# A decoder block in fp32: the FFN's result is transposed from its SBUF tiles, and operands of the last stage are asked for earlier

## The chip, the cores and the metric

The kernel runs on one core of a Trainium2 chip. The metric is the device time of one execution in microseconds; the median of several timed runs counts. Times inside an execution come from one profiled run and are counted from the start of its span.

## The reference

One layer of a hybrid decoder, sequence length 2048, width 1024, FFN width 2816, one batch, all fp32. The change lies behind the mixing part, in the last five lines.

```python
u = rmsnorm(h, attn_pre_norm)
... # gated linear recurrence and stick-breaking attention
h = h + rmsnorm(mix, attn_post_norm)
u = rmsnorm(h, ffn_pre_norm)
gate, up = split(u @ w_gate_up, [D_FF])
y = (silu(gate) * up) @ w_down
h = h + rmsnorm(y, ffn_post_norm)                 # called h2 below
out = h + (p @ ple_proj) * sigmoid(h @ ple_gate)  # called PLE below
```

## The kernel before

Every fp32 product is made of three matmuls of split operands: each operand `raw` is cast on ScalarE to a high part (`wh`, `uh`) and a low part `raw - high` is made on VectorE or GpSimd (`wl`, `ul`); `mm3` (lines 223 to 225) multiplies high by high, high by low, low by high. Tokens stand in four groups of 512 (0 to 3), a group in four token tiles of 128. The FFN and PLE matrix products work on a pair of groups at a time, with a scheme of seven block products in place of eight (`CHAIN`, in the order 1, 2, 6, 3, 7, 5, 4), so every operand exists as seven sums or differences of blocks.

`Drive` runs six stages one after the other: gate/up for groups 0 and 1 (stage 0), down (1), gate/up for groups 2 and 3 (2), down (3), PLE for groups 0 and 1 (4, the first PLE stage or first half) and PLE for groups 2 and 3 (5, the second half). A down stage has 77 steps of 12 matmuls, a gate/up stage 77 of 24, a PLE stage 36 of 12: seven products of four steps, then eight steps (`run_p`) that multiply `pt` by `ple_proj`. Before a step's matmuls, `Drive` has already issued the loads and casts (`prepare`) of steps 3 to 5 ahead. A hook `at(stage, step, f)` issues `f` right behind the matmuls of that step.

The order on TensorE is that of the code, word for word. On the other engines a scheduler fixes it when the program is built; at run time each engine takes its instructions in that order, so one that waits holds all behind it. Every DMA is issued by SyncE (SP in the rows). All loads of the last five stages go into one ring of ten buffers of 256 KB (`wr`, `load`, line 764).

Around the change:
- In a down stage, product 5 completes the result of the even group (0, 2) at step 65, product 4 that of the odd one (1, 3) at step 76. `ready[g][i]` holds the two halves of token tile `i`, SBUF tiles named `c` or `cu`.
- `post_y(g, i)` (line 1040) makes h2 of one token tile in place: sum of squares on ScalarE, 1/rms on GpSimd, scale by `gy` (a broadcast load of `ffn_post_norm`) on VectorE (line 1046), addition of the residual `hr` on GpSimd (line 789 by `add`), write to `h2_s` (line 1049; the rows print it `h_s`). It is hooked at stage 1 from step 67, stage 2 from step 0, stage 3 from step 67 and stage 4 from step 0.
- `turn` (line 696) loads rows of `h2_s` again (line 703, four blocks of 256 columns), transposes 128x128 blocks on TensorE (line 715), four to a PSUM bank `hg`, copies the bank on ScalarE (line 719) and writes 512 tokens of one feature block to `h2t_s` (line 722). Groups 0 and 1 are turned in stage 2, group 2 at stage 4 from step 2, group 3 from step 11.
- `s_part` (line 874) reads `h2t_s` and makes the operands of the second PLE half: part 0 those of products 1, 2 and 6, part 1 the other four. It is hooked at stage 4, steps 21, 23, 25, 27 (part 0) and 28 to 31 (part 1).
- `prepare_p` loads `ple_proj` and `pt`, and its casts need buffers `w` (eight in all) that the products before them still use.

Of the kernel before, what the change touches and what calls it, by code (L numbers as in the profile page):

```python
# [15 lines left out]
P = 128  # L16
T = 2048
D = 1024
ND = D // P
GT = 512  # L20
NG = T // GT
TT = GT // P
# [66 lines left out]
def hybrid_block(  # L89
# [6 lines left out]
    nc = tc.nc  # L96
    ctx.enter_context(tc.manual_schedule(engines={mybir.EngineType.PE}))
    x, p, out = x[0], p[0, 0], out[0]
# [6 lines left out]
    def scratch(name, shape):  # L105
        return [dram.tile(list(shape), F32, tag=f"{name}{g}", name=f"{name}{g}") for g in range(NG)]
# [9 lines left out]
    h2_s = scratch("h2_s", (GT, D))  # L116
    un_s = scratch("un_s", (GT, D))
    u_s = scratch("u_s", (ND, P, GT))
    h2t_s = scratch("h2t_s", (ND, P, GT))
# [9 lines left out]
    def ctile(name, shape, dt=F32, pool=const):  # L129
        return pool.tile(list(shape), dt, tag=name, name=name)  # L130

    ident = ctile("ident", (P, P))
# [40 lines left out]
    def bank(tag):  # L173
        return ps.tile([P, 512], F32, tag=tag, name=tag, bufs=BANKS[tag])
# [97 lines left out]
    def row_rstd(halves):  # L272
        ss = const.tile([P, 2], F32, tag="ss", name="ss", bufs=8)
        for j, y in enumerate(halves):
            nc.scalar.activation(junk, y, AF.Square, accum_out=ss[:, j:j + 1])
        r = const.tile([P, 1], F32, tag="ssum", name="ssum", bufs=8)
        nc.gpsimd.tensor_tensor(r, ss[:, 0:1], ss[:, 1:2], op=ALU.add)
        return rstd_of(const, r, D)
# [417 lines left out]
    def turn(src, dst, gain, tag, new_in, new_out):  # L696

        def get(q):
            ts = []
            for i in range(2):  # L700
                r = new_in().rearrange("p (t d) -> p t d", t=2)
                rows = src[2 * i * P:2 * (i + 1) * P, q * 256:(q + 1) * 256]
                nc.sync.dma_start(r, rows.rearrange("(t p) d -> p t d", p=P))
                ts += [r[:, 0, :], r[:, 1, :]]
            return ts

        nxt = get(0)
        yield
        for q in range(4):
            ts = nxt  # L710
            nxt = get(q + 1) if q < 3 else None
            for c in range(2):
                b = bank(tag)
                for t in range(TT):
                    nc.tensor.transpose(b[:, t * P:(t + 1) * P], ts[t][:, c * P:(c + 1) * P], ident)
                e = new_out()
                k = 2 * q + c
                if gain is None:
                    nc.scalar.copy(e, b)
                else:  # L720
                    nc.scalar.activation(e, b, AF.Copy, scale=gain[:, k:k + 1])
                nc.sync.dma_start(dst[k], e)
                yield
# [36 lines left out]
    def slot(tag, side, name, dt=F32):  # L760
        side = side if big[side] is not None else 0
        return big[side].tile([P, GT], dt, tag=f"{tag}{side}", name=name, bufs=SLOTS[tag.rstrip("hl")][side])

    def load(src, shape=None):
        r = slot("wr", 0, "wr")
        nc.sync.dma_start(r if shape is None else shape(r), src)
        return r

    def acc(name="acc"):
        turns["acc"] += 1  # L770
        return slot("acc", 0 if turns["acc"] % 3 == 0 else 1, name)

    def pair_of(src, kind, prod, lo_engine):
        if kind == "u":
            side = 0 if prod in (1, 2, 6) else 1
        else:
            turns["w"] += 1
            side = turns["w"] % 2
        hi = slot(kind + "h", side, kind + "h", F32R)
        lo = slot(kind + "l", side, kind + "l", F32R)  # L780
        nc.scalar.copy(hi, src)  # L781
        lo_engine.tensor_tensor(lo, src, hi.bitcast(F32), op=ALU.subtract)  # L782
        return hi, lo

    def sub(e, o, a, b):
        e.tensor_tensor(o, a, b, op=ALU.subtract)  # L786

    def add(e, o, a, b):
        e.tensor_tensor(o, a, b, op=ALU.add)  # L789
# [67 lines left out]
    def s_blk(grp, i, j, k):  # L857
        return load(h2t_s[2 * grp + i][4 * j + k])
# [15 lines left out]
    def s_part(grp, ss, part, k):  # L874

        a11, a12, a21, a22 = (s_blk(grp, i, j, k) for i, j in ((0, 0), (0, 1), (1, 0), (1, 1)))
        if part == 0:
            ss[1, k] = pair_of(a11, "u", 1, G)
            ss[2, k] = pair_of(a12, "u", 2, V)
            add(V, a21, a21, a22)  # L880
            sub(V, a21, a21, a11)
            ss[6, k] = pair_of(a21, "u", 6, V)
        else:
            ss[4, k] = pair_of(a22, "u", 4, G)
            add(V, a22, a21, a22)
            sub(V, a21, a11, a21)
            sub(V, a11, a22, a11)
            sub(V, a12, a12, a11)
            for prod, a, e in ((3, a12, V), (7, a21, V), (5, a22, G)):
                ss[prod, k] = pair_of(a, "u", prod, e)  # L890
# [113 lines left out]
    ready = {}  # L1004
# [35 lines left out]
    def post_y(g, i):  # L1040
        halves = ready[g][i]
        r = row_rstd(halves)
        for j, t in enumerate(halves):
            cs = slice(j * GT, (j + 1) * GT)
            gy = load(ffn_post_norm[0:1][:, cs].to_broadcast((P, GT)))
            nc.vector.scalar_tensor_tensor(t, t, r, gy, op0=ALU.mult, op1=ALU.mult)
            hr = load(h_s[g][i * P:(i + 1) * P, cs])
            add(G, t, t, hr)
            nc.sync.dma_start(h2_s[g][i * P:(i + 1) * P, cs], t)


    def ple(grp, ss):
        g0 = 2 * grp
# [111 lines left out]
    for n, (kind, g, att_n, hg_n) in enumerate(plan):  # L1165
        slots = IN_A if kind == "a" else IN_B
        main = Stream(in_proj(g, us[g], KQV if kind == "a" else HG))
        hg = {2: 0, 3: 0, 4: 1, 5: 1, 6: 2}.get(n)
        hg = hgs[hg] if hg is not None else idle
# [21 lines left out]
    tt0, tt1, ss0, ss1 = {}, {}, {}, {}  # L1191
# [46 lines left out]
    def at(stage, step, f):  # L1238
        hooks.setdefault((stage, step), []).append(f)

    def spread(stage, step, gen, n, every=1):
        st = Stream(gen)
        for i in range(n):
            at(stage, step + i * every, st.step)
# [4 lines left out]
    def turner(src, dst, gain):  # L1249
        return turn(src, dst, gain, "hg", wr, acc)  # L1250
# [11 lines left out]
        at(2, 10 + 16 * k, lambda k=k: ple_combos(k))  # L1262
        spread(3, 3 + 18 * k, s_all(0, ss0, k), 9, 2)
    for g in range(NG):
        stage, step = ((1, 67), (2, 0), (3, 67), (4, 0))[g]
        for i in range(TT):
            at(stage, step + (2 * i if g % 2 == 0 else i), lambda g=g, i=i: post_y(g, i))
    for i, g in enumerate((0, 1)):
        spread(2, 21 + 20 * i, turner(h2_s[g], h2t_s[g], None), 9, 2)
    for i, g in enumerate((2, 3)):  # L1270
        spread(4, 2 + 9 * i, turner(h2_s[g], h2t_s[g], None), 9)
    for i in range(2):
        for k in range(ND // 2):
            at(4, 21 + 7 * i + 2 * k - i * k, lambda i=i, k=k: s_part(1, ss1, i, k))
    drive.run(hooks)


# [25 lines left out]
```

## Time and profile before

| | us |
|---|---|
| timed runs, median of 3 | 3108.03 (3103.41 to 3109.69) |
| profiled execution | 3112.12 |
| its span | 3110.3 |
| TensorE busy in it | 2918.1 (94%) |
| VectorE / ScalarE / GpSimd busy | 2034.7 / 1584.4 / 1632.3 |

The span is what the trace covers; the profiled execution's time has some 2 us around it. PE is TensorE's matmul row, DVE VectorE, ACT ScalarE, POOL GpSimd, SPq SyncE's DMA queue. Matmuls are pipelined: a row's duration overlaps the next one, so that work is counted from start to start. Where an engine was idle before an instruction, the row ends with the idle time and what ended it.

### The profile page before, as it was taken

The numbers are of one execution on the slowest core, as the hardware profiler recorded it, in microseconds if no ns is written. First come the engines' busy times: TensorE is split into PE (matmuls) and PEld (weight loads), VectorE is DVE, ScalarE is ACT, GpSimd is POOL, SyncE is SP. The second block draws the span as 40 slices with busy tenths as digits, with TensorE's granted clock in tenths as the row PEclk, the third lists the DMA queues.
The fourth block names the chain that finished last, engine by engine and source line by source line (L and its number), as shares of the span: only waits on it lengthen the run. The fifth ranks groups of instructions, "written<-read, shape, count | busy, mean of one in ns | idle before, by whom it ended". The sixth has DMA issues, their size and how long they took to land. (4 is left out here: it accounts for less than half of the span.)

```text
span 3110.3 us, 52961 instructions
## 1 busy us (share of the span) xinstructions
PE 2918.1 (94%) x18280; PEld 2440.2 (78%) x18280; DVE 2034.7 (65%) x2801; ACT 1584.4 (51%) x3180; POOL 1632.3 (52%) x1606
## 2 busy tenths in 40 slices
PE   8999999999999999876879999999999999998979
PEld 7888787878787878776768787888788888887757
DVE  3555667677667766643786677846786676656474
ACT  5666656666667666754542333455333333545432
POOL 3344455545556666855644454555743343648364
PEclk9999999999999999998989999999999999999989
DMA  7765564555445443556666777677855664778784
GB/s 214 222 204 162 161 191 142 148 160 162 140 137 166 137 143 112 188 185 229 219 202 218 231 243 236 217 223 217 291 190 190 200 210 134 230 213 284 248 259 149
DMA packets 463822, 607.02 MB, mean 195 GB/s; under 512 B 43456, under 2 KB 269760, under 8 KB 463552
## 3 DMA queue, kind: packets, MB, share of 16 engines
q1 hardware_dynamic: 463552, 603.63, 62.2%
q8 instruction: 144, 2.36, 0.3%
q14 instruction: 126, 1.03, 0.1%
HBM read 444.61 MB, written 158.86 MB: 194 GB/s over the span
## 5 line engine op out<-in xcount | busy, mean ns | idle before, releaser
L781 ACT CAST wh<-wr 128x512 fp32r<-128x512 f32 x600 | 354.0, 619 | 558.8 <-PE mm L224 175.4
L782 POOL TENSOR_TENSOR wl<-wr,wh 128x512 fp32r<-128x512 f32 x256 | 370.5, 1454 | 369.6 <-ACT wh L781 360.4
L433 POOL TENSOR_TENSOR a<-be,ring 128x512 f32<-128x512 f32 (+2 forms) x320 | 318.8, 997 | 432.4 <-DVE ring L429 405.5
L223 PE MATMUL mm<-uh,wh 128*128 128x512 f32 x1168 | 483.1, 414 | 3.4 <-DVE vv L348 2.5
L225 PE MATMUL mm<-uh,wl 128*128 128x512 f32 x1168 | 459.3, 393 | 1.6 <-POOL wl L782 1.6
L224 PE MATMUL mm<-ul,wh 128*128 128x512 f32 x1168 | 458.6, 393 | 0.0
L782 DVE TENSOR_TENSOR wl<-wr,wh 128x512 fp32r<-128x512 f32 x344 | 314.1, 919 | 167.3 <-ACT wh L781 145.6
L429 DVE TENSOR_TENSOR_SCAN ring<-z,ring,be 128x512 f32<-128x512 f32 x192 | 245.7, 1280 | 116.5 <-ACT z L415 112.6
L223 PE MATMUL mm<-wh,uh 128*128 128x256 f32 (+1 forms) x992 | 309.7, 312 | 2.3 <-ACT wh L781 2.2
L224 PE MATMUL mm<-wl,uh 128*128 128x256 f32 (+1 forms) x992 | 294.0, 296 | 2.9 <-POOL wl L782 2.6
L225 PE MATMUL mm<-wh,ul 128*128 128x256 f32 (+1 forms) x992 | 292.9, 295 | 0.0
L225 PEld LDWEIGHTS mm<-uh,wl 128*128 128x128 f32 x1168 | 220.5, 189 | 51.2 <-POOL wl L782 2.0
L223 PEld LDWEIGHTS mm<-uh,wh 128*128 128x128 f32 x1168 | 221.7, 190 | 44.6 <-issue 2.6
L446 DVE TENSOR_TENSOR al<-tr,ah 128x512 fp32r<-128x512 f32 (+1 forms) x320 | 192.1, 600 | 91.6 <-ACT ah L444 91.1
L224 PEld LDWEIGHTS mm<-ul,wh 128*128 128x128 f32 x1168 | 221.6, 190 | 38.2
L210 POOL TENSOR_TENSOR wl<-wr,wh 128x512 fp32r<-128x512 f32 x144 | 188.9, 1312 | 117.3 <-ACT wh L209 111.5
L209 ACT CAST wh<-wr 128x512 fp32r<-128x512 f32 x288 | 178.0, 618 | 140.9 <-PE mm L224 83.5
L444 ACT CAST ah<-tr 128x512 fp32r<-128x512 f32 (+1 forms) x320 | 167.5, 523 | 109.9 <-PE tr L441 107.2
L414 ACT ACTIVATE be<-z 128x512 f32<-128x512 f32 (+2 forms) x320 | 171.1, 535 | 92.7 <-PE z L408 40.9
L223 PEld LDWEIGHTS mm<-wh,uh 128*128 128x128 f32 x992 | 191.7, 193 | 10.7 <-ACT wh L781 3.1
L224 PEld LDWEIGHTS mm<-wl,uh 128*128 128x128 f32 x992 | 192.2, 194 | 8.7 <-POOL wl L782 3.6
L225 PEld LDWEIGHTS mm<-wh,ul 128*128 128x128 f32 x992 | 191.7, 193 | 3.8
(289 smaller groups left out, 7307.3 us busy)
## 6 DMA issues: line engine op xcount, KB each, us to landing
wr<-in_w_gate_up_dram SPq DMA_DIRECT2D x308, 256.0 KB, 3.8
wr<-in_w_in_dram SPq DMA_DIRECT2D x224, 256.0 KB, 3.2
wr<-hid_s SPq DMA_DIRECT2D x154, 256.0 KB, 3.1
wr<-in_w_down_dram SPq DMA_DIRECT2D x110, 256.0 KB, 3.1
wr<-h_s SPq DMA_DIRECT2D x96, 256.0 KB, 3.8
hid_s<-hs SPq DMA_DIRECT2D x88, 256.0 KB, 2.9
wr<-wd_s SPq DMA_DIRECT2D x88, 256.0 KB, 3.5
kt<-k_s SPq DMA_DIRECT2D x80, 256.0 KB, 3.0
```

Of the source, the lines that this page charges most:

```text
L209: nc.scalar.copy(hi, src)
L210: (lo_engine or nc.gpsimd).tensor_tensor(lo, src, hi.bitcast(F32), op=ALU.subtract)
L223: nc.tensor.matmul(o, l[0], r[0], start=start, stop=False)
L224: nc.tensor.matmul(o, l[0], r[1], start=False, stop=False)
L225: nc.tensor.matmul(o, l[1], r[0], start=False, stop=stop)
L414: nc.scalar.activation(be[:, :n], z[:, :n], AF.Sigmoid, scale=0.125)
L429: nc.vector.tensor_tensor_scan(r[:, o:o + n][:, ::-1], z[:, :n][:, ::-1], be[:, :n][:, ::-1], init, op0=ALU.mult, op1=ALU.bypass)
L433: nc.gpsimd.tensor_tensor(a[:, :n], be[:, :n], r[:, o + 1:o + n + 1], op=ALU.mult)
L444: nc.scalar.copy(hi[:, lo_c:], tr[:, lo_c:])
L446: nc.vector.tensor_tensor(lo[:, lo_c:], tr[:, lo_c:], hi[:, lo_c:].bitcast(F32), op=ALU.subtract)
L781: nc.scalar.copy(hi, src)
L782: lo_engine.tensor_tensor(lo, src, hi.bitcast(F32), op=ALU.subtract)
```

## The change

`turn` is no longer used for h2. A new function `turn_y` transposes the SBUF tiles of one token tile, which `post_y` has just finished, and writes 128 tokens of four feature blocks at once. It is hooked 2 to 4 steps behind the `post_y` of its tile, with its PSUM banks from `mm` in the down stages and from `hg` elsewhere. The hooks of `s_part` move to steps 13, 15, 17, 19 (part 0) and 26 to 29 (part 1).

```diff
+    def turn_y(g, i, tag):
+
+        for j, t in enumerate(ready[g][i]):
+            b = bank(tag)
+            for c in range(TT):
+                nc.tensor.transpose(b[:, c * P:(c + 1) * P], t[:, c * P:(c + 1) * P], ident)
+            e = acc("ht")
+            nc.scalar.copy(e, b)
+            nc.sync.dma_start(
+                h2t_s[g][TT * j:TT * (j + 1), :, i * P:(i + 1) * P].rearrange("k p t -> p k t"),
+                e.rearrange("p (k t) -> p k t", k=TT))
+
...
     for g in range(NG):
-        stage, step = ((1, 67), (2, 0), (3, 67), (4, 0))[g]
+        stage, step, every, lag, tag = (
+            (1, 67, 2, 3, "mm"), (2, 0, 1, 2, "hg"), (3, 67, 2, 3, "mm"), (4, 0, 1, 4, "hg"))[g]
         for i in range(TT):
-            at(stage, step + (2 * i if g % 2 == 0 else i), lambda g=g, i=i: post_y(g, i))
-    for i, g in enumerate((0, 1)):
-        spread(2, 21 + 20 * i, turner(h2_s[g], h2t_s[g], None), 9, 2)
-    for i, g in enumerate((2, 3)):
-        spread(4, 2 + 9 * i, turner(h2_s[g], h2t_s[g], None), 9)
-    for i in range(2):
-        for k in range(ND // 2):
-            at(4, 21 + 7 * i + 2 * k - i * k, lambda i=i, k=k: s_part(1, ss1, i, k))
+            at(stage, step + i * every, lambda g=g, i=i: post_y(g, i))
+        for i in range(TT):
+            at(stage, step + i * every + lag, lambda g=g, i=i, tag=tag: turn_y(g, i, tag))
+    for k in range(ND // 2):
+        at(4, 13 + 2 * k, lambda k=k: s_part(1, ss1, 0, k))
+        at(4, 26 + k, lambda k=k: s_part(1, ss1, 1, k))
```

On TensorE, at the first transposes of the first PLE stage, before the change (`wr` holds reloaded rows of group 2; `av`, `tr` and `mm` are banks of product 1):

```order
L223 MATMUL av<-wh,uh 128x512
L224 MATMUL av<-wl,uh 128x512
L225 MATMUL av<-wh,ul 128x512
L715 MATMUL hg<-ident,wr 128x128 x4
L223 MATMUL tr<-wh,uh 128x512
```

and at the first transposes of that stage now (`cu` and `c_32009` are the two halves of token tile 0 of group 3):

```order
L225 MATMUL tr<-wh,ul 128x512
L1056 MATMUL hg<-ident,cu 128x128 x4
L1056 MATMUL hg<-ident,c_32009 128x128 x4
L223 MATMUL mm<-wh,uh 128x512
L224 MATMUL mm<-wl,uh 128x512
```

The transposes of this stage go from sixteen single groups, one behind each step from step 3 on, to four pairs behind steps 4 to 7; group 2's stand in the down stage ahead of it.

On SyncE, in the same stage, before the change, while `post_y` of group 3 runs (`h_s_94` is h2 of group 3, `h_s_93` that of group 2, `h_s_90` the residual of group 3, `wp_s` weights of PLE products):

```order
L1049 DMA h_s_94<-cu 128x512
L703 DMA wr<-h_s_93 128x2x256 x2
L1049 DMA h_s_94<-c_32041 128x512
L766 DMA wr<-wp_s_246 128x512
L766 DMA wr<-wp_s_247 128x512
L1049 DMA h_s_94<-cu 128x512
L766 DMA wr<-wp_s_248 128x512
L766 DMA wr<-wp_s_249 128x512
L1049 DMA h_s_94<-c_32047 128x512
L766 DMA wr<-in_ffn_post_norm_dram 128x512
L766 DMA wr<-h_s_90 128x512
```

and now, a little later in the same stage, up to the first reads of `h2t_s_105` and `h2t_s_106` (groups 2 and 3):

```order
L1049 DMA h_s_94<-cu 128x512
L766 DMA wr<-wp_s_249 128x512
L1059 DMA h2t_s_106<-ht 128x4x128
L766 DMA wr<-h2t_s_105 128x512
L1059 DMA h2t_s_106<-ht 128x4x128
L1049 DMA h_s_94<-c_32027 128x512
L766 DMA wr<-h2t_s_105 128x512
L1059 DMA h2t_s_106<-ht 128x4x128 x2
L766 DMA wr<-h2t_s_106 128x512 x2
L766 DMA wr<-wp_s_246 128x512
```

The reloads (L703) are gone from between the writes of h2 and the loads of the next tiles, and the reads of h2t for the second half stand among and right behind the last writes of h2t of group 3.

## Rows read from the trace of the kernel before

**Rows 1.** The page's 40 slices: TensorE's busy tenths and its granted clock.
```profile
PE   8999999999999999876879999999999999998979
PEclk9999999999999999998989999999999999999989
```

**Rows 2.** Stretches: length, busy PE, PEld, DVE, ACT, POOL (instructions), PEclk, DMA share, GB/s.
```profile
2203.80:2230.00 26.20, 19.38 (x73) 15.20 (x73) 23.16 (x27) 13.37 (x30) 21.17 (x22) 0.87 0.88 287
...
2853.80:3110.30 256.50, 220.73 (x929) 176.46 (x927) 150.40 (x176) 91.58 (x168) 130.71 (x101) 0.91 0.70 229
...
2853.80:2864.80 11.00, 11.00 (x49) 8.79 (x47) 9.29 (x10) 7.36 (x19) 9.36 (x10) 1.00 1.01 360
...
2892.00:2955.30 63.30, 63.07 (x300) 51.54 (x299) 33.42 (x40) 28.98 (x51) 20.32 (x15) 1.00 0.71 223
```

**Rows 3.** TensorE in time order, PLE stages: start, duration, instruction, idle before and releaser.
```profile
2853.76 0.39 PE L223 MATMUL mm<-wh,uh 128*128 128x512 f32 x1
...
2856.48 0.39 PE L223 MATMUL z<-wh,uh 128*128 128x512 f32 x1
...
2872.47 1.30 PE L715 MATMUL hg<-ident,wr 128*128 128x128 f32 x4 [7.67 <-DMA wr<-h_s]
...
2873.99 0.63 PE L224 MATMUL tr<-wl,uh 128*128 128x512 f32 x1
2874.42 0.63 PE L225 MATMUL tr<-wh,ul 128*128 128x512 f32 x1
...
2878.27 0.60 PE L715 MATMUL hg<-ident,wr 128*128 128x128 f32 x4
2878.63 0.48 PE L223 MATMUL mm<-wh,uh 128*128 128x512 f32 x1
...
3104.76 0.39 PE L225 MATMUL av<-wh,wl 128*128 128x512 f32 x1
```

**Rows 4.** TensorE's waits, PLE stages, then 2203.8 to 2240: total us, times, longest.
```profile
PE hg L715 <- DMA wr<-h_s: 11.1, 2, 7.7
PE mm L223 <- ACT wh L781: 7.2, 3, 5.1
PE z L224 <- POOL wl L782: 4.9, 1, 4.9
PE mm L224 <- POOL wl L782: 2.6, 1, 2.6
PE z L223 <- ACT wh L781: 2.0, 1, 2.0
PE mm L225 <- DVE wl L782: 1.6, 1, 1.6
...
PE tr L225 <- DVE wl L782: 5.2, 1, 5.2
PE mm L225 <- POOL wl L782: 1.6, 1, 1.6
```

**Rows 5.** GpSimd in time order: last addition of group 2, last of group 3.
```profile
2856.82 1.29 POOL L789 TENSOR_TENSOR c<-c,wr 128x512 f32<-128x512 f32 x1 [0.62 <-DVE c L1046]
...
2883.70 1.26 POOL L789 TENSOR_TENSOR c<-c,wr 128x512 f32<-128x512 f32 x1 [1.12 <-DMA wr<-h_s]
```

**Rows 6.** SyncE in time order: first reloads of group 2, first h2t reads.
```profile
2866.73 2.12 SPq L703 DMA_DIRECT2D wr<-h_s  x2
...
2923.25 0.96 SPq L766 DMA_DIRECT2D wr<-h2t_s  x2
```

**Rows 7.** DMA issues: size each and median us to landing.
```profile
kt<-k_s SPq DMA_DIRECT2D x80, 256.0 KB, 3.0
vt<-v_s SPq DMA_DIRECT2D x80, 256.0 KB, 3.3
```

**Rows 8.** ScalarE in time order ahead of the wait for `pt`.
```profile
2957.32 1.67 ACT L781 CAST uh<-wr 128x512 fp32r<-128x512 f32 x3 [0.45 <-DVE wr L786]
...
2959.82 0.60 ACT L781 CAST wh<-wr 128x512 fp32r<-128x512 f32 x1
```

## The prediction

> **What bounds the kernel now.** I read the slices first: TensorE is busy in nine tenths of nearly every slice, and the granted clock dips in few places, one of them the last tenth of the span [rows 1]. So a gain must come from stretches in which TensorE waits or runs at 1.2 GHz. The table of stretches shows where these lie for the lines that change: in the two PLE stages (2853.8 us to the end) TensorE is busy for 220.73 of 256.5 us at a mean granted clock of 0.91, and in the first 26 us of the second gate/up stage for 19.38 of 26.2 us at 0.87 [rows 2].
>
> How much the PLE stages lose follows from a count. Both halves together have 2 x 36 steps of 12 matmuls, 864. Between waits 12 of them take 2.72 us (start to start, 2853.76 to 2856.48), 0.2267 each; after a wait they come 0.43 apart, which is the 1.2 GHz level [rows 3]. The 16 groups of four transposes take 0.36 each, from the start of one to the next matmul [rows 3]. Without a wait that is 864 x 0.2267 + 16 x 0.36 = 201.6 us. The last matmul starts at 3104.76 [rows 3], so with its 0.23 some 251.2 us pass, and **about 50 us are lost**. The list of waits accounts for 30.2 us of them: 11.1 for reloaded rows of h2 that the transposes read, 19.1 for weights (`wh`, `wl`), of which five rows carry 18.3 and two smaller ones 0.8 [rows 4]. The other 20 us are matmuls at 1.2 GHz behind those waits: after the first transposes' wait 11 matmuls and a transpose group lose 11 x 0.2 + 0.7 = 2.9 us; for the second I take the same. So the transposes' waits cost 11.1 + 5.8 = 17 us, and the weights' waits 50 - 17 = 33 us.
>
> **Part 1: transposes from the tiles.** Removed are 32 reloads of 256 KB; 128 transposes, 32 evictions on ScalarE and 32 writes of h2t stay. In the PLE stage the reloads hold TensorE twice (the first wait ends at 2872.47 us [rows 3]): SyncE issues two reloads at 2866.73 [rows 6], and the rest come as late. The new transposes need no reload, but they stand in TensorE's fixed order behind the chain square, 1/rms, scale, add of their token tile, so the GpSimd add becomes their releaser.
> - *Token group 2* (end of the second down stage). The last step's matmuls end at 2853.76; six transpose groups ahead of the last tile push that to 2853.76 + 6 x 0.36 = 2855.9. The adds of tile 3 end at 2858.1 (2856.82 + 1.29) [rows 5]. Its residual load now also stands behind two h2t writes on SyncE; I allow 0.7 for it. So I expect a wait of 2.9, and 2.1 us for a slow clock behind it, 5 in all; bounds 0 (tiles ready) and 10 (the 7.7 of the longest present wait, plus slow matmuls) [rows 4].
> - *Token group 3* (PLE steps 4 to 7). TensorE would come to tile 3 at about 2855.9 + 2.9 + 8 x 2.72 + 8 x 0.36 = 2883.4. Its add ends at 2885.0 in the trace [rows 5], but there its scale and residual loads were issued behind the reloads and the h2 writes that SyncE waited for. Without them they leave some 2 us sooner. I take 1 us, bounds 0 and 6.5 (one present wait of 3.4 plus 3 us of slow clock).
> - *Groups 0 and 1* (end of the first down stage, start of the second gate/up). TensorE waits here for weights, 5.2 and 1.6 us [rows 4], and DVE, which makes these weights, is in its scales and combinations, not behind TensorE. Eight transpose groups (2.9 us) now stand ahead of that wait, so they are hidden in it: the 16 groups that ran later at full cost lose 2.9 us there. Against it stand copies of the transposed tiles in ScalarE's queue, up to 1 us later for the weights. I take a gain of 3, bounds a loss of 6 (ScalarE's copies, which wait for TensorE, hold the casts queued behind them) and a gain of 9 (both waits gone with their slow matmuls).
> - *The writes* change from 2 KB runs to runs of 512 B, 128x4x128. Nothing in the trace writes in this form; the loads of v_s have it and land in 3.3 us, the loads of k_s with 2 KB runs in 3.0 [rows 7]. The DMA engines are full at the start of the PLE stage (share 1.01 [rows 2]), where 4 MB of reloads go away, so I count nothing, with 0 to 2 us as bounds.
>
> The Trainium skill (DMA: Bandwidth & Descriptors, "Why small descriptors are slow") gives each packet a fixed overhead of about 3 cycles beside one cycle per 32 bytes. From that page I estimate 19 cycles for 512 B and 4 x 19 = 76 against 67 for 2 KB, 13% more DMA time per write; the pair of rows shows 10%. By it the sum would be some 2 us worse while the engines are full, instead of 0.
>
> **Part 2: operands of the second half sooner.** The first reads of h2t for this begin at 2923.25 us, asked for at step 21 of the first PLE stage [rows 6]. Everything that prepares weights then queues behind it: the cast of `pt`, for which TensorE waits 5.1 us, starts at 2959.82, and three casts of `uh` that had waited for DVE stand just before it [rows 8]; the weights of the second half come late from there on. Now part 0 is asked for at step 13 and part 1 at 26 instead of 28. The steps begin about 5 us later on the clock, but the waits of 17 us before step 13 are gone, so reads start near 2890, over 30 us sooner, and no longer end behind the last transposes of both groups. DVE's and ScalarE's work is the same amount; it is shifted into steps 13 to 24, where DVE is busy for about half (33.42 of 63.3 us [rows 2]). Two costs stay: the cast of `pt` needs a weight buffer that is freed in step 27, and the ring of ten load buffers still couples PLE weights, residual loads and h2t loads.
> - *The wait for `pt`*, now 5.1 + 1.6 us and about 1.8 of slow clock (8.5): I leave 2.
> - *The weights of products 1 and 2 of the second half*, the other 24.5 us: in the new order part 1's four blocks are all asked for before these weights, before three of four. So I take half of it, 12, as still lost; bounds 0 and 24.5.
>
> **The sum.** Lost now in the PLE stages: 50. Still lost: 5 + 1 + 2 + 12 = 20. Net 30, plus 3 at groups 0 and 1: 33 us. The profiled execution took 3112.1 us in all (2 beyond its span), so 3079; it was 4 above the median of the timed runs, 3108.0, so I forecast **3075 us** there.
>
> **Rivals.**
> 1. *Only the first part pays* (a transfer that stays late). The operand work is bound by the ring and by DVE, whose casts, sums and evictions interleave; starting sooner only lengthens it, and the 33 us stay. Then the gain is 17 - 6 + 3 = 14: 3094, or 3089 to 3101. For it: the ring holds ten buffers, and ple_proj and pt sit in six of them until their slots come free. Against it: DVE is half idle where the work goes. This is also the case in which the change does not do what it says for its second half.
> 2. *All waits go.* Nothing of the 20 us remains: 3055 to 3060. Against it: at least the last tile of group 2 is late by the trace's own times.
> 3. *The add is a worse wait than the reload*, slower than before. All 16 token tiles now have their transposes in TensorE's fixed order directly behind the GpSimd add, and GpSimd's queue interleaves these adds with weights (`wl`) that wait for casts. A wait of 3.4 us with 3 us of slow clock at a tile, as the second one now, would cost 16 x 6.4 = 102. What the change can gain apart from this is 33 + 6 = 39, so it decides from 2.4 us a tile on; at 3.2 a tile the time is 3108 + 12 = 3120. For it: tile 3 of group 2 and tile 0 of group 1 are near the limit. Against it: tiles 0 to 2 are ready before TensorE arrives, by the same reckoning.
> 4. *No change*: waits at the turns eat the gain within 6 us, 3108. It needs rival 3 at half its force and rival 1 at once.
>
> **How the numbers follow.** The forecast gets 0.60 (3062 to 3089), rival 1 0.20, rival 2 0.10, rival 3 0.06, rival 4 0.04. About 0.2%, 6 us, is what a measurement of this kernel can tell from no change; the first three cases lie beyond it, so faster 0.90, same 0.04, slower 0.06. The range runs from the lower end of rival 2 to most of rival 1: 3054 to 3098; it leaves out rivals 3 and 4, the rest of rival 1 and a little below.
>
> **What would show it.** In the changed profile there are no reloads of h2 rows and no TensorE wait on them. Right would be: waits of the new transposes on GpSimd adds under 8 us in all, the largest at tile 3 of group 2; the first h2t reads of the second half before 2900; less than 3 us of wait for `pt`; a mean granted clock above 0.95 in the PLE stages; the wait of 5.2 us at the start of the second gate/up stage smaller. Part 2 is wrong if waits for `wh` and `wl` at products 1 and 2 of the second half again come to over 10 us, and part 1 is wrong if transposes wait over 15 us on adds or on PSUM banks that ScalarE has not emptied.

## The result and the profile after

The changed kernel takes **3086.4 us** (median of 6 runs, 3085.5 to 3093.5); the kernel before took 3109.6 in its 6 runs by then. The ratio is 0.9935, 95% interval 0.9923 to 0.9948: faster by 0.5 to 0.8%, 20 us by the ratio and 23.2 between the medians. The forecast was 3075 with a range of 3054 to 3098, so the time lies inside, near the upper end of the forecast's own band (3062 to 3089), on the side of rival 1 (3094).

The profiled execution took 3085.75, with a span of 3084.0; that is 26.4 less than the profiled execution before (3112.12). Part of this is not the change's. The last transposes of `pt` (line 739) stand in the first gate/up stage, long ahead of everything that the change touches. The view of that line, kernel before and then after (duration min/median/max in ns, first and last start):

```profile
L739 PE MATMUL hg<-ident,wr x32: 270/272/472, 1874.2 to 1961.0; 128*128 128x128 f32 x32
```

```profile
L739 PE MATMUL hg<-ident,wr x32: 270/272/475, 1872.5 to 1957.8; 128*128 128x128 f32 x32
```

So 3.2 us of the 26.4 were there before the change began. From here to the last matmul's start I call it the *tail*: 3104.76 [rows 3] - 1961.0 = 1143.8 before, 3078.39 - 1957.8 = 1120.6 after, **23.2 us** less. All runs below are compared by it. A second profiled execution of the changed kernel (e11 below) has a tail of 1123.0. With one profiled execution of every other kernel, differences under some 3 us in the tail say nothing.

The slices of the page after, which answer to [rows 1]; the last tenths are full but for one:

```profile
PE   8999999999999999886879999999999999999989
PEclk9999999999999999998989999999999999999999
```

The table of stretches after (length, busy PE, PEld, DVE, ACT, POOL with instructions, granted clock, DMA share, GB/s), against [rows 2]: the start of the second gate/up stage, the PLE stages from the last step of the down stage on, and their first 11 us.

```profile
2203.40:2229.60 26.20, 20.30 (x81) 15.76 (x80) 22.13 (x27) 13.26 (x31) 17.28 (x20) 0.87 0.92 303
2852.30:3084.00 231.70, 208.29 (x906) 168.93 (x904) 143.50 (x177) 88.00 (x162) 129.92 (x101) 0.97 0.68 233
2852.30:2863.30 11.00, 7.12 (x29) 5.57 (x28) 8.20 (x10) 7.02 (x18) 8.41 (x12) 0.84 1.06 359
```

The PLE stages are 25 us shorter at a mean granted clock of 0.97 instead of 0.91. The start of the second gate/up stage has hardly changed (20.3 busy for 19.4, clock 0.87 as before), and a new dip stands at the head of the PLE stages.

The list of TensorE's waits after (total us, times, longest), PLE stages and then from 2200 to 2262, against [rows 4]:

```profile
PE mm L223 <- ACT wh L781: 5.3, 1, 5.3
PE mm L1056 <- POOL c L789: 3.9, 2, 2.4
PE hg L1056 <- ACT ht L1058: 3.1, 4, 0.8
PE mm L224 <- DVE wl L782: 2.9, 1, 2.9
PE z L224 <- POOL wl L782: 1.4, 1, 1.4
PE mm L224 <- POOL wl L782: 1.2, 2, 0.9
...
PE tr L225 <- DVE wl L782: 4.0, 1, 4.0
PE hg L1056 <- ACT ht L1058: 3.1, 4, 0.8
PE tr L223 <- ACT wh L781: 1.9, 1, 1.9
```

The 11.1 us on reloads are gone; 3.9 us on additions have come, 3.1 us in each of two stages on ScalarE's copy of a transposed bank (a wait that the kernel before did not have here), and one long wait for `pt` has stayed. TensorE in time order shows each (start, duration, instruction, idle before and releaser):

```profile
2855.09 0.66 PE L1056 MATMUL mm<-ident,c 128*128 128x128 f32 x4 [2.41 <-POOL c L789]
2857.21 1.12 PE L1056 MATMUL mm<-ident,c 128*128 128x128 f32 x4 [1.46 <-POOL c L789]
2857.98 0.78 PE L223 MATMUL mm<-wh,uh 128*128 128x512 f32 x1
2858.55 0.63 PE L224 MATMUL mm<-wl,uh 128*128 128x512 f32 x1
...
2872.69 0.60 PE L1056 MATMUL hg<-ident,cu 128*128 128x128 f32 x4
2874.05 0.63 PE L1056 MATMUL hg<-ident,c 128*128 128x128 f32 x4 [0.77 <-ACT ht L1058]
...
2942.60 0.39 PE L225 MATMUL z<-wh,ul 128*128 128x512 f32 x1
2948.30 0.80 PE L223 MATMUL mm<-wh 128*128 128x512 f32 x1 [5.31 <-ACT wh L781]
...
3078.39 0.39 PE L225 MATMUL av<-wh,wl 128*128 128x512 f32 x1
```

For the account I take the *loss* at a place: what the starts there lie apart beyond 0.2267 us for a matmul and 0.36 for a group of transposes [rows 3], so waits and the slow matmuls behind them. In us, with the second execution of the changed kernel:

| place | before | forecast | after | again |
|---|---|---|---|---|
| reloads (before) | 17.5 | 0 | 0 | 0 |
| last tile of group 2 | - | 5 | 5.8 | 6.6 |
| group 3's transposes | - | 1 | 4.1 | 4.1 |
| `pt` | 9.1 | 2 | 7.8 | 8.3 |
| weights, second half's products | 20.8 | 12 | 8.0 | 11.1 |
| sum | 47.4 | 20 | 25.7 | 30.1 |

What the column of before lacks to the prediction's 50 (49.6 by this count) is 0.09 at each of the old transpose groups and small gaps. From the last transposes of `pt` to the end of the second down stage it took 892.5 us before, 894.5 and 892.6 after, though 2.2 us of group 2's transposes moved there: a gain of 0.2 to 2.1 at groups 0 and 1.

### The profile page after: what moved, and what is told of

It reads as the page before. It is cut to its first block, busy times and chain, and to the rows that moved or that the text cites. A ratio compares the mean times of both kernels' runs of the same rounds, so it can differ in the third digit from the quotient of the medians.

```text
span 3084.0 us, 52907 instructions
## 1 busy us (share of the span) xinstructions
PE 2908.2 (94%) x18280; PEld 2435.1 (79%) x18280; DVE 2039.1 (66%) x2801; ACT 1583.5 (51%) x3180; POOL 1619.4 (53%) x1606
```

## The experiments

Each edit is to the changed kernel; the diffs show the lines that matter. Tail as above; losses in us; "weights" is the second half's products. "Part 1" alone means part 1 of the operands (`s_part`); the change's own two parts are called the transposes and the operand steps.

| kernel | tail | last tile | `pt` | weights | median | ratio, interval |
|---|---|---|---|---|---|---|
| before | 1143.8 | - | 9.1 | 20.8 | 3109.6 | 1 |
| changed | 1120.6 | 5.8 | 7.8 | 8.0 | 3086.4 | 0.9935, 0.9923 to 0.9948 |
| e11 changed again | 1123.0 | 6.6 | 8.3 | 11.1 | 3088.7 | 0.9943, 0.9930 to 0.9957 |
| e1 old operand steps | 1127.5 | 6.0 | 4.3 | 20.5 | 3093.2 | 0.9942, 0.9922 to 0.9961 |
| e2 halves apart | 1117.8 | 7.3 | 12.0 | 9.1 | 3083.0 | 0.9911, 0.9893 to 0.9929 |
| e3 part 1 at 32 to 35 | 1115.1 | 3.2 | 0 | 14.1 | 3087.1 | 0.9922, 0.9897 to 0.9946 |
| e4 with reloads | 1123.9 | 3.2 | 3.1 | 18.5 | 3090.8 | 0.9935, 0.9918 to 0.9952 |
| e5 groups 0, 1 old | 1124.1 | 5.2 | 8.5 | 10.7 | 3089.1 | 0.9940, 0.9925 to 0.9955 |
| e6 last tile one stage on | 1121.2 | 7.1 | 7.8 | 9.6 | 3092.6 | 0.9947, 0.9931 to 0.9963 |
| e7 three edits | 1112.3 | 8.6 | 0 | 14.5 | 3077.6 | 0.9897, 0.9881 to 0.9913 |
| e8 part 1 in second half | 1111.1 | 9.1 | 0 | 12.9 | 3077.2 | 0.9895, 0.9880 to 0.9911 |
| e9 part 1 spread | 1119.7 | 6.7 | 0 | 16.0 | 3084.1 | 0.9918, 0.9904 to 0.9933 |
| e10 spread, halves, tile | 1106.0 | 0.5 | 0 | 13.5 | 3073.0 | 0.9888, 0.9871 to 0.9904 |
| e12 no residual loads | 1120.5 | 6.1 | 7.9 | 8.0 | 3090.4 | 0.9933, 0.9913 to 0.9952 |

### What is the second part worth? (e1, e11)

```diff
-        at(4, 13 + 2 * k, lambda k=k: s_part(1, ss1, 0, k))
-        at(4, 26 + k, lambda k=k: s_part(1, ss1, 1, k))
+        at(4, 21 + 2 * k, lambda k=k: s_part(1, ss1, 0, k))
+        at(4, 28 + k, lambda k=k: s_part(1, ss1, 1, k))
```

> The changed kernel with the second half's operand steps put back to 21, 23, 25, 27 and 28 to 31; the transposes stay as changed. Measured for the change: 3086.4. In its trace the PLE stages lose 26 us where the kernel before loses 49; 16.9 of the gain of 23 is at weights (pt and products 1, 2 of the second half), the rest at the transposes. Theory A (the earlier operand steps bring the gain at the weights): these losses come back, 15 to 17 us, and the time is 3101 to 3104, with the wait for pt and the waits at products 1 and 2 as in the kernel before (some 33 us lost there). Theory B (the weights come sooner because 32 reloads are gone from the load ring and from SyncE; the earlier steps add little): the loss at the weights stays near 16 us and the time within 3 us of 3086. By my prediction (part 2 worth 19 of 33) it would be 19 above 3086, 3105.

> The changed kernel once more, to see how far one profiled execution stands for the kernel. From the last transposes of the first gate/up stage to the last matmul it took 1120.6; if the waits are set by the program's order alone it is 1120.6 within 1, and the difference between executions lies ahead of that point. If the waits at the weights move by themselves it differs by 3 or more, and differences below that say nothing.

Neither theory's number came. The tail is 1127.5, 4.5 to 6.9 more than in the two executions with the earlier steps, and the median 4.5 to 6.8 more; the ratios with their intervals can't tell the two apart. So by these executions the transposes alone give 16.3 us of the tail (1143.8 - 1127.5), and the earlier operand steps 5 to 7, not 19. Theory A's 15 to 17 took the loss at the weights before for 33; by the table it is 29.9, and 14.1 of it had gone. The repeat's tail is 2.4 longer: 4.4 more by the places of the table, 3.1 of it at the second half's weights, and 1.9 less ahead of the PLE stages. So those waits do move by themselves. The waits of e1 say where (PLE stages; the weights' rows):

```profile
PE z L224 <- POOL wl L782: 5.9, 2, 4.9
PE mm L223 <- ACT wh L781: 4.4, 2, 2.4
...
PE mm L224 <- POOL wl L782: 3.4, 2, 2.5
...
PE z L223 <- ACT wh L781: 1.5, 1, 1.5
```

The longest wait for `pt` is 2.4 here, half of that before [rows 4] with the same operand steps: the transposes from the tiles halved this loss (9.1 to 4.3), while the loss at the products' weights stayed (20.8 and 20.5). With the earlier steps it is back at 7.8 and 8.3, while the loss at the products' weights falls from 20.5 to 8.0 and 11.1.

### Is `pt` held by part 1? (e3)

```diff
-        at(4, 26 + k, lambda k=k: s_part(1, ss1, 1, k))
+        at(4, 32 + k, lambda k=k: s_part(1, ss1, 1, k))
```

ScalarE of the changed kernel in time order, ahead of TensorE's 5.31 us, shows the suspicion: `pt`'s cast `wh` behind a cast of part 1 that waits for its h2t load. The load is one of part 1's second quarter, which SyncE issued in the last row.

```profile
2946.59 0.62 ACT L781 CAST uh<-wr 128x512 fp32r<-128x512 f32 x1 [3.32 <-DMA wr<-h2t_s]
2947.12 0.62 ACT L1100 ACTIVATE cu<-cu 128x512 f32<-128x512 f32 x1
2947.65 0.60 ACT L781 CAST wh<-wr 128x512 fp32r<-128x512 f32 x1
...
2938.53 3.83 SPq L766 DMA_DIRECT2D wr<-h2t_s  x4
```

> The changed kernel with part 1 of the second half's operands at steps 32 to 35 instead of 26 to 29, so behind the loads and casts of pt for both halves. In the changed kernel the cast of pt starts at 2947.65 on ScalarE, directly behind a cast uh that waited 3.3 us for its h2t load, and TensorE waits 5.3 us for it, then loses 2.5 us more (7.8). Theory A (part 1's loads and casts stand ahead of pt in the load ring and in ScalarE's order, that is why the wait stayed): the wait for pt falls below 1 us and these 7.8 us go; the weights of products 1 and 2 of the second half, 8.1 us lost now, then stand among part 1's work and may lose up to 4 more: 3078 to 3083. Theory B (pt is held by the weight buffers, which step 27 frees): the wait for pt stays at 5 us, time 3086 or above.

The wait for `pt` is gone, theory A. The waits in the PLE stages of e3:

```profile
PE z L224 <- POOL wl L782: 4.9, 2, 3.8
PE z L223 <- ACT wh L781: 3.1, 2, 1.7
...
PE mm L224 <- POOL wl L782: 1.0, 1, 1.0
```

But the products' weights now lose 14.1 instead of 8.0 or 11.1, so of 8 us some 3 to 6 are given back, and the timed runs (3079.7 to 3092.3) show no gain that stands out. 2.6 of the tail's 5.5 us came at the last tile of group 2, which this edit does not touch.

In e1 other casts stood ahead of `pt`'s. ScalarE, then SyncE's last reads of part 0 and first of part 1:

```profile
2945.62 0.62 ACT L781 CAST uh<-wr 128x512 fp32r<-128x512 f32 x1 [0.53 <-DMA wr<-h2t_s]
...
2949.52 0.61 ACT L781 CAST wh<-wr 128x512 fp32r<-128x512 f32 x1
...
2940.76 2.77 SPq L766 DMA_DIRECT2D wr<-h2t_s  x4
...
2947.00 3.69 SPq L766 DMA_DIRECT2D wr<-h2t_s  x4
```

Part 1's first reads were issued at 2947.00, after that cast of `uh`, so it is one of part 0's last quarter, and its wait was 0.53 instead of 3.32 us.

### Does part 1's cost move with it? (e8, e9, e12)

e8 puts part 1 at steps 0 to 3 of the second half (with the edits of e7, below), e9 at four steps three apart; e12 leaves out the first half's residual loads and adds the gated product to itself in their place. The lines of e8 and e9 stand in place of the one that e3 changes; the labels behind # are not in the code.

```diff
+        at(5, k, lambda k=k: s_part(1, ss1, 1, k))                              # e8
+        at(4 + (k > 1), (32, 35, 2, 5)[k], lambda k=k: s_part(1, ss1, 1, k))    # e9
```

```diff
-                hr = load(h2_s[g0 + half][i * P:(i + 1) * P, c])
-                add(G, y, y, hr)
+                if grp == 0:
+                    add(G, y, y, y)
+                else:
+                    ...
```

> As the kernel with three edits, but part 1 behind steps 0 to 3 of the second half (its first use is step 12), so behind the weights of products 1 and 2. Theory A (part 1's loads stand ahead of those weights in the load ring and its casts ahead of theirs): the 14 us lost at products 1 and 2 fall below 5, and the time is 5 to 9 below the kernel with three edits. Theory B (residual loads and weight buffers hold these weights, not part 1): the waits at products 1 and 2 stay, and product 6 or 3 gains a new one: no gain, or up to 5 slower.

> The changed kernel with part 1 of the second half's operands at steps 32 and 35 of the first PLE stage and 2 and 5 of the second: one step in three instead of four in a row. Counted from a fixed matmul to the last one the runs so far take 1120.6 (the change, part 1 at 26 to 29) and 1115.1 (at 32 to 35), and the kernel with part 1 at steps 0 to 3 of the second half loses as much at products 6 and 3 as the one at 32 to 35 does at products 1 and 2. Theory A (four steps in a row bring 16 loads and the casts for them at once; the weights behind them are late, whichever they are): spread out, the 14 us lost at the second half's weights fall to 4 or less, 1105, and the time is 3071. Theory B (part 1 costs the same queue time wherever it stands): 1113 to 1117, no difference to part 1 at 32 to 35.

> The changed kernel without the 16 residual loads of the first half: where it adds h2 (reloaded rows) to the gated product, it adds that product to itself, so the GpSimd additions stay and the first half's output lacks h2. In the changed kernel SyncE issues product 1's weights of the second half at 2967.6, behind residual loads that take turns with output writes, then six residual loads in 9.4 us, then product 2's weights from 2982.9. Theory A (these loads hold the ring of ten buffers and SyncE's queue, and so the weights behind them): the weights of products 1 and 2 are asked for 10 us sooner or more, and the 8.1 us lost there (11.1 in the second execution) fall below 3; the wait for pt, 7.8, whose cast stands behind part 1's h2t loads, may fall as well, by up to 5. From the last transposes of the first gate/up stage to the last matmul 1120.6 and 1123.0 become 1110 to 1116. Theory B (the casts and VectorE's sums of part 1 hold the weights): the waits stay within 3 us of 16 in all, 1118 to 1123.

In e8 products 1 and 2 lose only 0.9, but products 6 and 3 lose 12: theory B's new waits, with 1.2 us of gain in the tail. In e9 the loss is 16.0, with its largest wait now for product 3's operand itself:

```profile
PE mm L223 <- ACT uh L781: 6.2, 1, 6.2
```

Spreading gives nothing, as in theory B, though the tail of 1119.7 is longer than its 1113 to 1117. e12 asked for the weights of product 1 6 us sooner on the clock, 10 sooner counted from the last transposes of `pt` (1961.4 there), and the tail stayed at 1120.5, inside theory B's bounds. SyncE in time order, of the changed kernel and then of e12 (the reads of part 1, then product 1's weights):

```profile
2967.64 1.13 SPq L766 DMA_DIRECT2D wr<-in_ple_gate_dram  x2
2969.01 0.34 SPq L1106 DMA_DIRECT2D out_dram<-c  x1
2969.45 0.92 SPq L766 DMA_DIRECT2D wr<-in_ple_gate_dram  x2
2970.46 9.42 SPq L766 DMA_DIRECT2D wr<-h_s  x6
```

```profile
2942.61 15.27 SPq L766 DMA_DIRECT2D wr<-h2t_s  x11
...
2961.45 0.33 SPq L766 DMA_DIRECT2D wr<-in_ple_gate_dram  x1
```

Even without residual loads among them, eleven reads of part 1 take 15.3 us to issue. So it is not the residual loads that hold the weights. e12's one loss there, 8.0, is a wait of 5.97 us at product 1 for a low part that GpSimd made. TensorE, ScalarE and then GpSimd of e12:

```profile
2983.90 0.80 PE L224 MATMUL mm<-wl,uh 128*128 128x512 f32 x1 [5.97 <-POOL wl L782]
...
2972.51 2.19 ACT L781 CAST uh<-wr 128x512 fp32r<-128x512 f32 x4 [4.32 <-DVE wr L786]
...
2977.23 2.95 POOL L782 TENSOR_TENSOR ul<-wr,uh 128x512 fp32r<-128x512 f32 x2
...
2982.13 1.71 POOL L782 TENSOR_TENSOR wl<-wr,wh 128x512 fp32r<-128x512 f32 x1
```

The weight's cast stood right behind part 1's four casts on ScalarE and was done by 2975.8; its `wl` stood behind part 1's two `ul` and additions for the output on GpSimd. So here part 1's casts and low parts stood ahead of the weight, which fits theory B. What holds part 1's own reads (ring buffers that its casts and VectorE's sums give back late, or the slots of its operands) these runs do not separate.

### Is it the reload's traffic or its place? (e4)

```diff
+    for n, g in enumerate((2, 3)):
+        for q in range(4):
+            at(4, 2 + 9 * n + max(0, 2 * q - 1), lambda g=g, q=q: reload_rows(g, q))
```

`reload_rows` issues two of the loads of line 703, for no reader.

> The changed kernel with the 16 reloads of h2 rows of groups 2 and 3 kept in the first PLE stage as mere loads of 256 KB into the load ring, at the steps where they stood before (2, 3, 5, 7 and 11, 12, 14, 16); no one reads them. Theory A (it was the reload's place ahead of the transposes that cost, a dependence): the time is within 3 us of 3086, with waits on TensorE as in the changed kernel. Theory B (the traffic itself costs, through the ring of ten buffers and the full DMA engines at the start of that stage): the loads for group 3's tiles, for weights and the h2t reads come later, and 5 to 12 us are lost, 3091 to 3098.

The tail is 1123.9, 0.9 to 3.3 above the two executions without them, and the ratio 0.9935 is the changed kernel's. Theory A in the sum, within what can be told: sixteen loads of 256 KB more cost little, so the 17.5 came from TensorE's dependence on them. But the waits are not those of the changed kernel: `pt` loses 3.1 and the products' weights 18.5, in all 21.6 for 15.8 and 19.4. And e4's loads give their ring buffers back on landing, while those of the kernel before kept them until their transposes; no run shows what that keeping cost.

### The bank between two halves (e2)

```diff
+            if g % 2:
+                for j in range(2):
+                    at(stage, step + 2 * i + j + lag, lambda g=g, i=i, j=j, tag=tag: turn_y(g, i, tag, (j,)))
+                continue
```

`turn_y` now takes the halves to be turned; both still go through the one bank `hg`, a step apart.

> The changed kernel with the two halves of a token tile of groups 1 and 3 transposed behind two different steps, one bank each, at steps 2 to 9 of the second gate/up stage and 4 to 11 of the first PLE stage. In the changed kernel TensorE waits eight times, 0.77 to 0.81 us, for ScalarE's copy of the first half, since both halves go through the one bank hg. Theory A (this wait is a cost of its own on the path): all eight go, 8 x 0.8 = 6.3 us, and nothing comes instead: 3080. Theory B (in the second gate/up stage or the PLE stage TensorE runs into the next weights' wait anyway): half of it, the four of one stage, is given back: 3083. Theory C (the bank's wait is replaced by a wait of the same bank for the step's own work, or later operands): no change, 3086.

All eight waits on ScalarE's copy went. In the second gate/up stage the gain stayed (888.8 to the end of the second down stage, for 894.5 and 892.6); in the PLE stages the four came back at `pt`, where e2 waits 7.9 instead of 5.3:

```profile
PE mm L223 <- ACT wh L781: 7.9, 1, 7.9
```

This is theory B. That the loss at `pt` grows from 7.8 and 8.3 to 12.0, about what TensorE saves ahead of it, speaks for a cast of `pt` that does not follow TensorE there.

### Groups 0 and 1 (e5) and the last tile of group 2 (e6, e7, e10)

e5 takes groups 0 and 1 back to reloaded rows. e6 moves only the last tile of group 2:

```diff
+            if (g, i) == (2, 3):
+                at(4, 1, lambda: turn_y(2, 3, "hg"))
+                continue
```

e7 is e2, e3 and e6 together. e10 is e2 and e9 with the two halves of this tile behind steps 1 and 4 (group 3 from step 5 on).

> The changed kernel, but groups 0 and 1 transposed as before, from reloaded rows in the second gate/up stage; groups 2 and 3 and the operand steps as changed. My prediction gave the new transposes of groups 0 and 1 a gain of 3 us, hidden in a wait for weights at the start of that stage: then this kernel takes 3089. The traces of before and after say otherwise: from the end of the first gate/up stage's last transposes to the end of the second down stage 892.5 us before and 894.5 after, of which 2.2 are group 2's six transpose groups that moved there, so a gain of 0 to 0.5: then it takes 3086 to 3087, its waits at the start of that stage 5.2 and 1.6 us as before, and no waits for ScalarE's copies there.

> The changed kernel with the last token tile of group 2 transposed behind step 1 of the first PLE stage, through bank hg, not behind the last step of the down stage. In the changed kernel TensorE waits there 2.4 and 1.5 us for the GpSimd additions and loses 5.8 us with the slow matmuls behind. Theory A (the time is lost at that place alone): these 5.8 us go, one bank wait of 0.8 comes for them, 3081. Theory B (TensorE runs into the wait for pt, 7.8 us now, that much earlier, since pt's cast is not behind TensorE): the 5 us come back there, 3086, and the wait for pt grows from 5.3 to about 9.

> Three edits at once on the changed kernel: halves of a token tile of groups 1 and 3 behind two steps, part 1 of the second half's operands at steps 32 to 35, the last tile of group 2 behind step 1 of the first PLE stage. Counted from a fixed matmul, the halves alone gave 2.8 us (5 in the second gate/up stage, 3 given back at pt), the later part 1 alone 5.5. If the gains add where pt no longer waits: 5 + 3 (given back no more) + 5.5 + 5 (tile) = 18 below 3086, 3068. Rival: the weights of products 1 and 2 of the second half, 14 us lost when part 1 is late, do not follow TensorE and take 6 to 10 of it: 3074 to 3078.

> The spread part 1, the halves of groups 1 and 3 behind two steps each, and the two halves of the last tile of group 2 behind steps 1 and 4 of the first PLE stage (group 3's from step 5 on). In the runs with this tile behind step 1 TensorE waited 5.4 and 5.8 us between its two halves, for ScalarE's copy of the first, which stood behind the sums of squares of four token tiles of group 3. Theory A: three steps later that copy is done (it started 5.7 us after the first transposes), so nothing is lost there; 5.8 us of the change's loss there, 5.0 at the second gate/up stage's bank waits and 3 at those of group 3 go beside what the spread gives: 1120.6 - 14 - 12 = 1095 to 1101, time 3061 to 3067. Theory B (the order on ScalarE and GpSimd shifts again and a new wait of 4 to 8 us comes at that boundary): 1103 to 1107, time 3069 to 3073.

e5's tail is 1124.1, 1.1 to 3.5 longer: groups 0 and 1 from the tiles are worth 1 to 3 us there, about the forecast, but 0.2 to 2.1 by the two executions against before; below what can be told.

e6 missed both ways: the wait on additions went, and one as long came between the two halves, so nothing was gained. TensorE and then ScalarE of e6 in time order:

```profile
2860.42 0.60 PE L1056 MATMUL hg<-ident,c 128*128 128x128 f32 x4
2866.47 1.08 PE L1056 MATMUL hg<-ident,c 128*128 128x128 f32 x4 [5.44 <-POOL ssum L277]
...
2865.75 0.57 ACT L1058 COPY ht<-hg 128x512 f32<-128x512 f32 x1
```

The row names GpSimd, but the bank `hg` was empty only when ScalarE's copy, which stood behind seven of the eight squares for group 3's rms, was done at 2866.3; in e7 and e8 the same 5.8 us are put down to that copy. In e10 the second half stands three steps later, and the place loses 0.5 us:

```profile
2862.01 0.60 PE L1057 MATMUL hg<-ident,c 128*128 128x128 f32 x4
...
2870.66 0.60 PE L1057 MATMUL hg<-ident,c 128*128 128x128 f32 x4
...
2866.69 0.57 ACT L1059 COPY ht<-hg 128x512 f32<-128x512 f32 x1
```

e7 came out at its rival's 3074 to 3078. e10 has a tail of 1106.0, longer than theory A's 1095 to 1101 and inside theory B's 1103 to 1107. Yet B's new wait at that boundary did not come: theory A held for the tile, and the spread brought none of its 14 us. At 3073.0 and a ratio of 0.9888 (0.9871 to 0.9904) it is **faster than both kernels**: the changed kernel's intervals (0.9923 to 0.9948, 0.9930 to 0.9957) lie wholly above, the second against the same runs of the kernel before.

## Why the prediction was right, and where it was not

- *What bounds the kernel.* Right: waits and slow matmuls in the PLE stages, 49.6 us by the same count from the end of the down stage, forecast 50. Nearly all the gain is there.
- *The reloads' 17 us.* Right: 17.5 lost before, none after, and e4 shows that it was the dependence.
- *The last tile of group 2.* 5 forecast, 5.8 and 6.6 measured. The waits on additions are 3.9 in all, under the 8 that I named.
- *Group 3.* The step that failed is the reckoning that TensorE comes to tile 3 at 2883.4 and its add ends at 2885.0: it priced the add (1) and left out the bank. No add was waited for; both halves of a tile go through the one bank `hg`, and each second half waits 0.77 to 0.81 for ScalarE's copy, a loss of 4.1 us in the PLE stages; the same 3.1 us of waits came at group 1. The Trainium skill (Perfetto Trace Analysis, "Matmuls") says that independent groups should rotate through different PSUM banks so that ScalarE's evacuation overlaps the next group; the row of 2874.05 agrees: with one bank TensorE waited 0.77 us for the evacuation. No run here gives the halves two banks; e2 kept the one bank, put a step between them and had no such wait, but in the PLE stages what this gave was lost again at `pt`.
- *Groups 0 and 1.* The 2.9 us hidden in the weights' wait were not: the waits there went from 5.2 + 1.6 [rows 4] to 4.0 + 1.9, so the weights came later as well, and 3.1 us of bank waits came. 3 forecast, 0.2 to 2.1 measured.
- *The wait for `pt`.* The step that failed is "I leave 2". It rested on the first reads of h2t starting over 30 us sooner, which they did:

```profile
2886.80 0.52 SPq L766 DMA_DIRECT2D wr<-h2t_s  x1
```

  But the wait hangs on the last casts of `uh` ahead of `pt`'s on ScalarE, not on the first reads. Before and in e1 these are part 0's ([rows 8]; part 1's first read was issued at 2960.38 there): 9.1 and 4.3 lost. The change took part 0's away and put a cast of part 1's second quarter there, 7.8 and 8.3; with all of part 1 behind `pt` nothing is lost (e3). The hook step alone does not set it: in e4, with part 1 at 26 too, only its first quarter stood ahead, and 3.1 were lost, at a low part that VectorE made. I had read in [rows 8] that three casts of `uh` stood just ahead of `pt`'s, and did not ask what would take their place.
- *The weights of the second half.* 12 forecast, 8.0 and 11.1 measured, and by the earlier operand steps, since e1 loses 20.5.
- *The sum.* 33 forecast, 23 in the tail. By parts, 14 for the transposes in rival 1 and 16.3 in e1, of which 4.8 came at `pt`, where I had counted nothing for them; 19 for the operands' steps and 5 to 7 measured. This term was mis-sized most. That the median still lies in the forecast's band is in part the band's width: the next case, rival 1, begins at 3089. Rival 1 had the mechanism of the operand steps in part right ("starting sooner only lengthens it"): e3, e8 and e9 move the loss from one set of weights to the next and keep most of it. Its number was not: it left all 33 us at the weights, and 15.8 to 19.4 stayed. Rival 1's ring was not shown: e12 speaks against the residual loads' share in it.
- *The signs.* All that I named held (waits on additions, first reads, granted clock 0.97, a shorter wait at the second gate/up stage) but one: the wait for `pt` was 5.3, not under 3. The signs against the two parts did not come (5.5 us of waits at products 1 and 2, 10.1 of the transposes' waits), so they missed what e1 shows of the second part.
- *Rivals 2 to 4.* The waits did not all go: 25.7 and 30.1 us stayed in the places of the table. The additions were no worse wait: 3.9 us at one tile of sixteen.

## What to carry to other kernels

When work is asked for sooner, list what it now stands ahead of on each in-order queue: here part 1's casts moved in front of `pt`'s on ScalarE, and gave back 3.5 to 4 us of the 9.4 to 12.5 that the earlier start brought at the products' weights. Two transposes in a row through one PSUM bank cost a wait for the copy between them (0.8 us), and where that copy's engine has a burst of other work queued, the wait is as long as the burst (5.4 to 5.8 us); a few steps between them removed it. A saving ahead of a wait that does not follow the saving engine can be given back there, as at `pt` in e2, so look for such waits first.

## What the runs showed of the hardware that I had not expected

The start of the last transposes of `pt`, ahead of which the code of all these kernels is the same, varies between 1950.3 (e9) and 1965.0 us (e10) in the profiled executions. This is more than most differences that were asked for here, and comparing from a fixed instruction on takes it out: the two executions of the changed kernel agree within 2.4 there. What makes it vary stays open. And the new writes of h2t with 512 B runs land in 5.3 us (median of 16) from 2830 to 2895, no later than nearly all other transfers there (5.3 to 6.2; three reads of h2t 3.8), while the DMA engines are full (their packets fill 101.7% of that stretch); the extra cost of 0 to 2 us that I allowed for them does not show.
